# A two-block sequence model on one core: weight sums of the seven-product up projection formed by accumulating DMAs

## The chip, the cores and the metric

The kernel runs on one core of one Trainium2 chip. The metric is the device time of one execution in microseconds (us); several executions of one build are timed and the median is given. Engines are named as in the profile: PE (TensorE), PEld (its weight loads), DVE (VectorE), ACT (ScalarE), POOL (GpSimd), SP (SyncE); a "q" behind a name is that engine's queue of instructions, and DMAs are issued from the queues of SP, ACT and POOL.

## The reference

Two blocks of two layers each on 512 tokens of 1024 features, in float32. The first block has a recurrent layer and an attention layer, which the change doesn't touch. Each layer of the second block ends with the part that matters here, a feed-forward network with a squared ReLU:

```python
    x = x + merged @ w_o
    h2 = rmsnorm(x, norm_mlp)
    return x + jnp.square(jax.nn.relu(h2 @ w_up)) @ w_down
```

`w_up` is 1024 x 4096 and `w_down` 4096 x 1024, both float32, and there are two such layers.

## The kernel before

Every float32 operand is split into two float32r parts that add up to it (high part by an ACT copy, line 59 for weights; low part by a DVE subtraction, line 60), and every product is made of three matmuls (high x high, high x low, low x high; lines 254 to 256, `mm3`).

**Weights come as a stream** (`Stream`). An item is one output tile of 128 columns, [128, 1024] float32, 512 KB. It is loaded by SP into a tile of the pool `wraw` (4 buffers), split by ACT and DVE into tiles of `whi` and `wlo` (3 buffers each), and read by PE. A buffer comes free when its last reader is done.

**The up projection** of a layer makes 32 output tiles in 16 pairs. A pair takes seven products of half-size blocks in place of eight (Winograd's variant of Strassen's product): the two weight tiles are cut into four blocks, A11 and A12 (first tile, lower and upper half of the contraction), A21 and A22 (second tile). Besides A11, A12 and A22 as they are, four sums are wanted: S1 = A21 + A22, S2 = S1 - A11, S3 = A11 - A21, S4 = A12 - S2. `_emit_sums` forms them with four [128, 512] additions (lines 96, 98, 101 and 104): by POOL for the first four pairs of a layer (`pooled`), by DVE for the other twelve. S1, S2 and S4 stand in the pool `sraw` (2 buffers) and are split into the pool `sums` (tiles `sh`, `sl`, 3 buffers each); S3 overwrites A21 in its `wraw` tile. In names, the stream's number stands before the sum: `sr191S`, `sh191S`, `wr191a`, `wr191b`. The blocks of the activations, T1 to T4 (tiles TH, TL), xH and xL, come from the norm ahead of the up projection (`PairNorm`).

`pair` multiplies in the order A11, A12, S1, S2, S3, S4, A22 (products 1, 2, 5, 6, 7, 3, 4), twelve 256-column matmuls each, and recombines on ACT (copies, lines 395 and 397), DVE (lines 396, 398, 401, 402, 404, 406) and POOL (line 399, `s_up`: one 256-column addition for each pair, on which lines 402 and 404 wait). Behind it stand ReLU times the norm's row (line 1150, DVE), the square (line 1151, ACT) and the split into aH and aL (lines 269 and 270).

**Groups.** Four pairs and eight tiles of the down projection (`dn`, 512-column matmuls) make a group; a layer has four groups, the kernel eight. The first two down tiles multiply parts 0 to 5 of the contraction first (36 matmuls), and then parts 6 and 7, which the last pair makes.

**Order.** PE's order is written out by hand. The orders of the other engines, and of the DMAs on their queues, come from a list scheduler that works with its own estimates of time; each engine then runs its list strictly in that order, so that an instruction that waits holds all behind it. `W.next()` emits the weights of the pair after the one it returns (`ahead` is 1 for pairs).

Of the kernel before, what the change touches and what calls it, by code (L numbers as in the profile page):

```python
# [7 lines left out]
F32 = mybir.dt.float32  # L8
# [7 lines left out]
P = 128  # L16
S = 512
D = 1024
KD = D // P
EPS = 1e-6  # L20
# [10 lines left out]
# columns of the packed per-partition vectors  # L31
# [16 lines left out]
class Stream:  # L48
    """Weights in order of use: load, split into two float32r parts that add up exactly."""

    def __init__(self, tc, raw, hi, lo, items, ahead):
        self.nc, self.raw, self.hi, self.lo = tc.nc, raw, hi, lo
        self.items, self.ahead = items, ahead
        self.done, self.taken = [], 0
        self.sums = self.sraw = None
        self.pooled = 0  # so many of the next sums go to GpSimd, while VectorE has much else to do
# [5 lines left out]
    def _emit_sums(self, i, s1, s2):  # L62
        """Weights of two output tiles in Winograd's seven forms, each a pair of [P, 4, P] parts.

        Rows of the 2 x 2 blocks A are the output tiles, columns the halves of the contraction.
        """
        nc, hw, nh = self.nc, KD * P, KD * P // 2
        eng = nc.gpsimd if self.pooled > 0 else nc.vector
        self.pooled -= 1
        r1 = self.raw.tile([P, hw], F32, tag="wraw", name=f"wr{i}a")  # L70
        r2 = self.raw.tile([P, hw], F32, tag="wraw", name=f"wr{i}b")
        nc.sync.dma_start(r1, s1)
        nc.sync.dma_start(r2, s2)
        a11, a12, a21, a22 = r1[:, :nh], r1[:, nh:], r2[:, :nh], r2[:, nh:]
# [16 lines left out]
        def sraw(nm):  # L91
            return self.sraw.tile([P, nh], F32, tag="sraw", name=f"sr{i}{nm}")

        whole(("A11", "A12"), r1)
        v1 = sraw("S1")
        eng.tensor_add(v1, a21, a22)
        half("S1", v1)
        eng.tensor_sub(a21, a11, a21)
        whole(("S3", "A22"), r2)
        v2 = sraw("S2")  # L100
        eng.tensor_sub(v2, v1, a11)
        half("S2", v2)
        v4 = sraw("S4")
        eng.tensor_sub(v4, a12, v2)
        half("S4", v4)
# [35 lines left out]
class Map:  # L141
    """A pool whose tags stand for tags of other pools."""
# [9 lines left out]
def build(tc, A, out, dbg=None):  # L152
# [3 lines left out]
    with ctx:  # L156
# [116 lines left out]
        def rsqrt_row(dst, src, scale, tp, tag, load=True):  # L273
            """dst = 1 / sqrt(src * scale + EPS), all float32 of one shape: a first value and a Newton step."""
# [12 lines left out]
        def colsum(acc, tp, tag):  # L287
            """Sum of acc over its partitions, on every partition of a PSUM tile."""
# [8 lines left out]
        class Norm:  # L297
            """Splits x * gain as tiles of x come, and sums their squares."""
# [39 lines left out]
        class PairNorm:  # L338
            """As Norm, with Winograd's forms of x * gain: blocks are halves of the features by halves of the tokens."""
# [27 lines left out]
        def pair(tag, forms, cp, cs, first=False):  # L367
            """Two output tiles [P, S] by Winograd's variant of Strassen's product."""
# [12 lines left out]
            steps = ((1, "A11", "B11"), (2, "A12", "B21"), (5, "S1", "T1"), (6, "S2", "T2"))  # L381
# [16 lines left out]
            dve.tensor_add(z, ps[6], s1)  # L398
            pool.tensor_add(s5, s5, z)  # L399
            prod(7, "S3", "T3")  # L400
            dve.tensor_add(z, ps[7], z)
            dve.tensor_add(c2[:, S2:], ps[7], s5)
            prod(3, "S4", "B22")
            dve.tensor_add(c1[:, S2:], ps[3], s5)
            prod(4, "A22", "T4")
            dve.tensor_add(c2[:, :S2], ps[4], z)
# [10 lines left out]
        def columns(r, tag):  # L417
            """[P, 4]: the row r with tokens on partitions."""
# [7 lines left out]
        def log1p_small(dst, e, tp, shape, tag):  # L426
            """log(1 + e) for e in [0, 1], to float32 accuracy in relative terms."""
# [15 lines left out]
        def trig():  # L443
            """cos and sin of position * frequency, [frequency twice, token]: sin on partitions ..63, cos on 64.. first."""
# [23 lines left out]
            # rows 64.. multiply the second half into the first one  # L468
            act.mul(sind[64:], sind[:64], -1.0)

        # =====================================================================
        # layer 1: LRU
        # =====================================================================
        with ExitStack() as lc:
# [13 lines left out]
            # softplus(-a_param), times -4 and -8  # L488
# [132 lines left out]
        # =====================================================================  # L621
        # layer 2: forgetting attention
        # =====================================================================
        with ExitStack() as lc:
# [20 lines left out]
            # keys: high parts twice; low parts, and over the other half of the rows the cumulated forget gates  # L645
# [5 lines left out]
            def fox_forget(ft):  # L651
                """Log sigmoid of the forget gates, [token, block of tokens and head], in two parts."""
# [19 lines left out]
            # P^T of a head, key block kb from column 384 * kb + query on  # L672
# [187 lines left out]
        # =====================================================================  # L860
        # second block
        # =====================================================================
# [61 lines left out]
        for li in range(2):  # L924
# [254 lines left out]
            lay.close()  # L1179


# [1 line left out]
def lay_out(inputs):  # L1183
    import numpy as np

# [96 lines left out]
```

## Time and profile before

| | |
|---|---|
| time, median of 3 runs | 2293.59 us (2293.43 to 2295.14) |
| profiled execution | 2293.59 us, all of it inside its span of 2293.6 us |
| PE busy | 2238.3 us (98%) |
| DVE / ACT / POOL busy | 1543.9 (67%) / 1065.4 (46%) / 369.0 us (16%) |
| DMA | 210.42 MB, mean 92 GB/s, queue of SP 28.1% of the 16 engines |
| PE share of the chain that ended last | 82% |

Of a group of instructions the profile gives busy time, the mean of one, and the idle time of its engine just before with what ended that idle time. A DMA issue is given with its size and the time from issue to landing.

### The profile page before, as it was taken

The numbers are of one execution on the slowest core, as the hardware profiler recorded it, in microseconds if no ns is written. First come the engines' busy times: TensorE is split into PE (matmuls) and PEld (weight loads), VectorE is DVE, ScalarE is ACT, GpSimd is POOL, SyncE is SP. The second block draws the span as 40 slices with busy tenths as digits, with TensorE's granted clock in tenths as the row PEclk, the third lists the DMA queues.
The fourth block names the chain that finished last, engine by engine and source line by source line (L and its number), as shares of the span: only waits on it lengthen the run. The fifth ranks groups of instructions, "written<-read, shape, count | busy, mean of one in ns | idle before, by whom it ended". The sixth has DMA issues, their size and how long they took to land.

```text
span 2293.6 us, 30071 instructions
## 1 busy us (share of the span) xinstructions
PE 2238.3 (98%) x11818; PEld 1909.7 (83%) x11818; DVE 1543.9 (67%) x2256; ACT 1065.4 (46%) x1629; POOL 369.0 (16%) x269
## 2 busy tenths in 40 slices
PE   8898999999999999999999999999999999999998
PEld 6687778887888888887998998988888887998996
DVE  7987877777776445448875774766345548875774
ACT  5666577765556222235543444556222225443443
POOL 3434211113211000003310112211000004210112
PEclk9999999999999999999999999999999999999999
DMA  4133222222222332332332333222333322333331
GB/s 153 64 99 97 90 65 74 65 74 80 81 94 74 101 100 94 98 95 74 110 102 95 100 109 99 89 89 80 96 97 95 98 92 83 101 103 100 97 107 55
DMA packets 62509, 210.42 MB, mean 92 GB/s; under 512 B 6944, under 2 KB 11424, under 8 KB 62368
## 3 DMA queue, kind: packets, MB, share of 16 engines
q1 hardware_dynamic: 59552, 204.43, 28.1%
q10 hardware_dynamic: 2672, 3.81, 0.6%
q8 instruction: 93, 1.52, 0.3%
q14 instruction: 48, 0.39, 0.1%
q0 software_dynamic: 144, 0.26, 0.0%
HBM read 206.37 MB, written 2.10 MB: 91 GB/s over the span
## 4 chain that ended last, share of the span: by engine, by line
PE 82%; DVE 5%; ACT 1%; issue 1%; POOL 0%; DVEq 0%; ACTq 0%; POOLq 0%
PE dn L255 5%; PE dn L256 5%; PE dn L254 5%; PE up L255 4%; PE up L256 4%; PE up L254 4%; PE ro L981 1%; PE wr L256 1%; PE wc L254 1%; PE wc L256 1%; PE wc L255 1%; PE wr L255 1%; PE wr L254 1%; PE ga L254 1%; PE ga L256 1%
## 5 line engine op out<-in xcount | busy, mean ns | idle before, releaser
L59 ACT CAST wh<-wr 128x1024 fp32r<-128x1024 f32 (+2 forms) x332 | 337.2, 1017 | 707.9 <-PE dn L255 120.5
L60 DVE TENSOR_TENSOR wl<-wr,wh 128x1024 fp32r<-128x1024 f32 (+2 forms) x332 | 398.5, 1202 | 49.7 <-ACT wh L59 47.9
L255 PE MATMUL dn<-aL,wh 128*128 128x512 f32 x488 | 192.9, 395 | 0.3 <-DVE aL L270 0.3
L256 PE MATMUL dn<-aH,wl 128*128 128x512 f32 x488 | 192.8, 395 | 0.0
L254 PE MATMUL dn<-aH,wh 128*128 128x512 f32 x488 | 192.7, 395 | 0.0
L399 POOL TENSOR_TENSOR s_up<-s_up,sz_up 128x256 f32<-128x256 f32 x32 | 52.6, 1644 | 473.5 <-DVE sz_up L398 163.8
L1169 DVE TENSOR_TENSOR x<-dn,x 128x512 f32<-128x512 f32 x61 | 42.0, 689 | 111.1 <-PE dn L256 110.8
L255 PEld LDWEIGHTS dn<-aL,wh 128*128 128x128 f32 x488 | 91.5, 187 | 22.7 <-DVE aL L270 0.7
L256 PEld LDWEIGHTS dn<-aH,wl 128*128 128x128 f32 x488 | 91.5, 187 | 22.3
L254 PEld LDWEIGHTS dn<-aH,wh 128*128 128x128 f32 x488 | 91.5, 187 | 22.1
L326 POOL TENSOR_TENSOR nacc_m<-nacc_m,nsq_m 128x512 f32<-128x512 f32 x14 | 21.0, 1499 | 486.4 <-ACT nsq_m L325 486.4
L256 PE MATMUL rv<-wh,xL 128*128 128x256 f32 x256 | 72.4, 283 | 0.0
L255 PE MATMUL rv<-wl,xH 128*128 128x256 f32 x256 | 72.4, 283 | 0.0
L254 PE MATMUL rv<-wh,xH 128*128 128x256 f32 x256 | 72.4, 283 | 0.0
L1151 ACT ACTIVATE c_up<-c_up 128x512 f32<-128x512 f32 x64 | 40.5, 633 | 35.0 <-DVE c_up L1150 34.7
L254 PE MATMUL wo<-mH,wh 128*128 128x512 f32 x128 | 51.1, 399 | 0.0
L256 PE MATMUL wr<-yrH,wl 128*128 128x512 f32 x128 | 51.1, 399 | 0.0
L254 PE MATMUL wc<-zH,wh 128*128 128x512 f32 x128 | 50.6, 396 | 0.0
L256 PE MATMUL wc<-zH,wl 128*128 128x512 f32 x128 | 50.6, 395 | 0.0
L255 PE MATMUL wc<-zL,wh 128*128 128x512 f32 x128 | 50.5, 395 | 0.0
L255 PE MATMUL wr<-yrL,wh 128*128 128x512 f32 x128 | 50.5, 394 | 0.0
L256 PE MATMUL wo<-mH,wl 128*128 128x512 f32 x128 | 50.4, 394 | 0.0
(1561 smaller groups left out, 7144.5 us busy)
## 6 DMA issues: line engine op xcount, KB each, us to landing
wr<-in_w_in SPq DMA_DIRECT2D x112, 512.0 KB, 3.5
wr<-in_w_down SPq DMA_DIRECT2D x64, 512.0 KB, 3.5
wr<-in_fox_w_in SPq DMA_DIRECT2D x24, 512.0 KB, 3.5
wr<-in_lru_w_in SPq DMA_DIRECT2D x23, 512.0 KB, 3.6
wr<-in_w_v SPq DMA_DIRECT2D x16, 512.0 KB, 3.5
wr<-in_w_ret_out SPq DMA_DIRECT2D x16, 512.0 KB, 3.5
wr<-in_w_conv_out SPq DMA_DIRECT2D x16, 512.0 KB, 3.6
wr<-in_w_o SPq DMA_DIRECT2D x16, 512.0 KB, 3.5
```

Of the source, the lines that this page charges most:

```text
L59: self.nc.scalar.copy(h, src)
L60: self.nc.vector.tensor_sub(l, src, h.bitcast(F32))
L254: pe.matmul(ps, wH, aH, start=start, stop=False)
L255: pe.matmul(ps, wH, aL, start=False, stop=False)
L256: pe.matmul(ps, wL, aH, start=False, stop=stop)
L326: (dve if j > 5 and acc is self.acc2 else pool).tensor_add(acc, acc, sq)
L399: pool.tensor_add(s5, s5, z)
L981: pe.matmul(po[i][:, q0:], vp[:, kb, vs], sp_[:, so], start=n == 0, stop=n == 11)
L1151: act.activation(t, t, AF.Square)
L1169: dve.tensor_add(x[:, j], ps, x[:, j])
```

## The change

The four additions of a pair go away. The raw sums are formed while the weights are loaded: POOL issues DMAs that add their source onto a tile that is already in SBUF (`accum_op=add`). Since these only add, the second output tile is computed with its sign turned, so that all four sums are plain additions: V1 = A21 + A22, V3 = A21 + A11, V2 = A11 + V1, V4 = A12 + V2, and the recombination subtracts where it added. `sraw` has 3 buffers in place of 2, one each for V1, V2 and V4 of a pair. A pair now has five loads by SP (two of 512 KB, three of 256 KB) and four accumulating DMAs by POOL of 256 KB each; two of these read HBM (V1, V3), and two read the sum before them in SBUF (V2 reads V1, V4 reads V2). `pooled` is gone. The remaining lines of the diff take comments out, and shift line numbers behind `_emit_sums` by one.

```diff
@@ Stream._emit_sums
-        eng = nc.gpsimd if self.pooled > 0 else nc.vector
-        self.pooled -= 1
-        r1 = self.raw.tile([P, hw], F32, tag="wraw", name=f"wr{i}a")
-        r2 = self.raw.tile([P, hw], F32, tag="wraw", name=f"wr{i}b")
-        nc.sync.dma_start(r1, s1)
-        nc.sync.dma_start(r2, s2)
-        a11, a12, a21, a22 = r1[:, :nh], r1[:, nh:], r2[:, :nh], r2[:, nh:]
...
+        def load(nm, src):
+            t = self.sraw.tile([P, nh], F32, tag="sraw", name=f"sr{i}{nm}")
+            nc.sync.dma_start(t, src)
+            return t
+
+        add = mybir.AluOpType.add
+        r1 = self.raw.tile([P, hw], F32, tag="wraw", name=f"wr{i}a")
+        nc.sync.dma_start(r1, s1)
+        v1 = load("V1", s2[:, :nh])
+        nc.gpsimd.dma_start(v1, s2[:, nh:], accum_op=add)
+        r2 = self.raw.tile([P, hw], F32, tag="wraw", name=f"wr{i}b")
+        nc.sync.dma_start(r2, s2)
+        nc.gpsimd.dma_start(r2[:, :nh], s1[:, :nh], accum_op=add)
+        v2 = load("V2", s1[:, :nh])
+        nc.gpsimd.dma_start(v2, v1, accum_op=add)
+        v4 = load("V4", s1[:, nh:])
+        nc.gpsimd.dma_start(v4, v2, accum_op=add)
         whole(("A11", "A12"), r1)
-        v1 = sraw("S1")
-        eng.tensor_add(v1, a21, a22)
-        half("S1", v1)
-        eng.tensor_sub(a21, a11, a21)
-        whole(("S3", "A22"), r2)
-        v2 = sraw("S2")
-        eng.tensor_sub(v2, v1, a11)
-        half("S2", v2)
-        v4 = sraw("S4")
-        eng.tensor_sub(v4, a12, v2)
-        half("S4", v4)
+        half("V1", v1)
+        half("V2", v2)
+        whole(("V3", "A22"), r2)
+        half("V4", v4)
@@ pair
-            dve.tensor_add(z, ps[6], s1)
-            pool.tensor_add(s5, s5, z)
-            prod(7, "S3", "T3")
+            dve.tensor_sub(z, s1, ps[6])
+            pool.tensor_sub(s5, s5, z)
+            prod(7, "V3", "T3")
...
@@ build
-                W.pooled = 4
-                W.sraw = lay.enter_context(tc.tile_pool(name=f"u{li}_r", bufs=2, side="right"))
+                W.sraw = lay.enter_context(tc.tile_pool(name=f"u{li}_r", bufs=3, side="right"))
```

The change moves instructions on three engines. POOL first, in the second group of a layer (its pairs have the stream's numbers 189 to 192, the next group's first pair 201; `s_up_1_0`, `_2`, `_4`, `_6` are the additions of line 399 for its four pairs). Before:

```order
L399 TENSOR_TENSOR s_up_1_0_9934<-s_up_1_0_9934,sz_up_1_0_9935 128x256
L399 TENSOR_TENSOR s_up_1_2_10082<-s_up_1_2_10082,sz_up_1_2_10083 128x256
L399 TENSOR_TENSOR s_up_1_4_10230<-s_up_1_4_10230,sz_up_1_4_10231 128x256
L399 TENSOR_TENSOR s_up_1_6_10353<-s_up_1_6_10353,sz_up_1_6_10354 128x256
L399 TENSOR_TENSOR s_up_2_0_10782<-s_up_2_0_10782,sz_up_2_0_10783 128x256
```

Now, in the same place (L97 adds A11 onto `wr192b`, L94 forms V1, L99 V2, L101 V4):

```order
L400 TENSOR_TENSOR s_up_1_0_9952<-s_up_1_0_9952,sz_up_1_0_9953 128x256
L97 DMA wr192b<-in_w_up 128x512
L94 DMA sr191V_10018<-in_w_up 128x512
L99 DMA sr191V_10024<-sr191V_10018 128x512
L101 DMA sr191V_10027<-sr191V_10024 128x512
L400 TENSOR_TENSOR s_up_1_2_10103<-s_up_1_2_10103,sz_up_1_2_10104 128x256
L94 DMA sr192V_10169<-in_w_up 128x512
L99 DMA sr192V_10175<-sr192V_10169 128x512
L101 DMA sr192V_10178<-sr192V_10175 128x512
L400 TENSOR_TENSOR s_up_1_4_10254<-s_up_1_4_10254,sz_up_1_4_10255 128x256
L94 DMA sr201V_10641<-in_w_up 128x512
L99 DMA sr201V_10647<-sr201V_10641 128x512
```

POOL had one addition for each pair and nothing between; now three or four DMA issues stand between two of them, of which each waits for the DMA before it to land. The next row of POOL is `s_up_1_6`. The sums of pairs 189 and 190 stand ahead of these rows, in the time of the down projection before.

DVE in the same group, at its last pair (`c_up_1_6`; `sl201V` are low parts of the next group's first pair). Before:

```order
L398 TENSOR_TENSOR sz_up_1_6_10354<-up_1_6_6_10339,s_up_1_6_10352 128x256
L270 TENSOR_TENSOR aL_1_4_10285<-c_up_1_4_10232,aH_1_4_10284 128x512
L401 TENSOR_TENSOR sz_up_1_6_10354<-up_1_6_7_10362,sz_up_1_6_10354 128x256
L402 TENSOR_TENSOR c_up_1_6_10356<-up_1_6_7_10362,s_up_1_6_10353 128x256
L404 TENSOR_TENSOR c_up_1_6_10355<-up_1_6_3_10377,s_up_1_6_10353 128x256
```

Now:

```order
L399 TENSOR_TENSOR sz_up_1_6_10378<-s_up_1_6_10376,up_1_6_6_10363 128x256
L59 TENSOR_TENSOR sl201V_10658<-sr201V_10641,sh201V_10657 128x512
L59 TENSOR_TENSOR sl201V_10662<-sr201V_10647,sh201V_10661 128x512
L402 TENSOR_TENSOR sz_up_1_6_10378<-up_1_6_7_10386,sz_up_1_6_10378 128x256
L403 TENSOR_TENSOR c_up_1_6_10380<-s_up_1_6_10377,up_1_6_7_10386 128x256
L405 TENSOR_TENSOR c_up_1_6_10379<-up_1_6_3_10401,s_up_1_6_10377 128x256
```

The splits of the next group's V1 and V2 have moved ahead of the last pair's recombination.

SP in the same stretch. Before:

```order
L73 DMA wr191b<-in_w_up 128x1024
L72 DMA wr192a<-in_w_up 128x1024
L73 DMA wr192b<-in_w_up 128x1024
L120 DMA wr_10294<-in_w_down 128x1024
L120 DMA wr_10417<-in_w_down 128x1024
```

Now:

```order
L92 DMA wr192a<-in_w_up 128x1024
L96 DMA wr192b<-in_w_up 128x1024
L87 DMA sr191V_10018<-in_w_up 128x512
L87 DMA sr191V_10024<-in_w_up 128x512
L87 DMA sr191V_10027<-in_w_up 128x512
L121 DMA wr_10318<-in_w_down 128x1024
L121 DMA wr_10441<-in_w_down 128x1024
L87 DMA sr192V_10169<-in_w_up 128x512
```

Three loads of 256 KB for each pair have come in, behind the loads of the tiles that the pair after it needs whole and among those of the down projection.

## Rows read from the trace of the kernel before

**Rows 1.** The page: busy time of each engine over the span.

```profile
PE 2238.3 (98%) x11818; PEld 1909.7 (83%) x11818; DVE 1543.9 (67%) x2256; ACT 1065.4 (46%) x1629; POOL 369.0 (16%) x269
```

**Rows 2.** Waits of PE, 1040 to 1460 us (engine, line, releaser: total, times, longest).

```profile
PE up L255 <- DVE xL L270: 2.2, 2, 1.4
PE up L254 <- ACT xH L269: 2.1, 1, 2.1
```

**Rows 3.** Windows: one group's pairs and downs (busy by engine, clock, DMA share, GB/s).

```profile
1167.78:1207.65 39.87, 39.87 (x338) 39.87 (x336) 36.20 (x62) 23.13 (x37) 7.23 (x4) 1.00 0.34 106
1207.65:1252.44 44.79, 44.79 (x194) 35.98 (x193) 23.46 (x31) 12.61 (x16) 0.00 (x0) 1.00 0.29 94
```

**Rows 4.** Timeline of PE: first matmuls of pairs 1 and 2, first of the downs.

```profile
1167.78 0.28 PE L254 MATMUL up<-xH,wh189A 128*128 128x256 f32 x1
...
1177.75 0.28 PE L254 MATMUL up<-xH,wh190A 128*128 128x256 f32 x1
...
1207.65 0.39 PE L254 MATMUL dn<-aH,wh 128*128 128x512 f32 x1
```

**Rows 5.** Timeline of DVE in that group (start, length, line, tiles, idle before).

```profile
1171.82 1.23 DVE L60 TENSOR_TENSOR wl190S<-wr190b,wh190S 128x1024 fp32r<-128x1024 f32 x1 [0.47 <-ACT wh190S L59]
...
1188.39 0.68 DVE L96 TENSOR_TENSOR sr192S<-wr192b 128x512 f32<-128x512 f32 x1
...
1198.99 0.42 DVE L401 TENSOR_TENSOR sz_up<-up,sz_up 128x256 f32<-128x256 f32 x1 [0.64 <-POOL s_up L399]
1199.33 0.41 DVE L402 TENSOR_TENSOR c_up<-up,s_up 128x256 f32<-128x256 f32 x1
1199.66 0.41 DVE L404 TENSOR_TENSOR c_up<-up,s_up 128x256 f32<-128x256 f32 x1
...
1201.46 0.68 DVE L60 TENSOR_TENSOR sl192S<-sr192S,sh192S 128x512 fp32r<-128x512 f32 x1
1202.06 0.68 DVE L1150 SCALAR_TENSOR_TENSOR c_up<-c_up,r_m 128x512 f32<-128x512 f32 x1
```

**Rows 6.** Timeline of POOL: sums of pair 177, and line 399 of pair 189.

```profile
1053.56 1.31 POOL L96 TENSOR_TENSOR sr177S<-wr177b 128x512 f32<-128x512 f32 x1 [2.43 <-DMA wr177b<-in_w_up]
1054.94 2.16 POOL L98 TENSOR_TENSOR wr177b<-wr177a,wr177b 128x512 f32<-128x512 f32 x1
...
1174.27 1.04 POOL L399 TENSOR_TENSOR s_up<-s_up,sz_up 128x256 f32<-128x256 f32 x1 [49.44 <-ACT sh190S L59]
```

**Rows 7.** Timeline of DVE ahead of the up projection and in its first products.

```profile
1074.46 1.78 DVE L270 TENSOR_TENSOR xL<-xgb_m,xH 128x512 fp32r<-128x512 f32 x1
...
1084.69 0.68 DVE L270 TENSOR_TENSOR xL<-xgb_m,xH 128x512 fp32r<-128x512 f32 x1
```

**Rows 8.** POOL's one DMA: time on the engine itself (ns min/median/max).

```profile
L643 POOL DMA_DIRECT2D tri<-in_tri x1: 741/741/741, 263.5 to 263.5; - x1
```

**Rows 9.** DMA issues (tiles, queue, count, KB each, us from issue to landing).

```profile
wr<-in_w_down SPq DMA_DIRECT2D x64, 512.0 KB, 3.5
...
wr<-in_lru_wab SPq DMA_DIRECT2D x12, 128.0 KB, 2.0
...
wr192b<-in_w_up SPq DMA_DIRECT2D x1, 512.0 KB, 4.4
...
wr<-in_fox_vf SPq DMA_DIRECT2D x1, 272.0 KB, 2.7
...
tri<-in_tri POOLq DMA_DIRECT2D x1, 256.0 KB, 3.2
```

**Rows 10.** Timeline of ACT in that group: split, square, split of the result.

```profile
1182.13 0.62 ACT L59 CAST sh191S<-sr191S 128x512 fp32r<-128x512 f32 x1 [0.37 <-PE up L255]
...
1182.92 0.64 ACT L1151 ACTIVATE c_up<-c_up 128x512 f32<-128x512 f32 x1
...
1184.08 0.62 ACT L269 CAST aH<-c_up 128x512 fp32r<-128x512 f32 x1
```

**Rows 11.** Timeline of DVE: waits on ACT of one dependency.

```profile
1163.27 1.22 DVE L60 TENSOR_TENSOR wl189S<-wr189b,wh189S 128x1024 fp32r<-128x1024 f32 x1 [0.20 <-ACT wh189S L59]
```

More of the change, by code (lines that the diff above doesn't have):

```diff
@@ L55, in __init__ @@
         self.sums = self.sraw = None
-        self.pooled = 0
     def _split(self, h, l, src):
@@ L89, in half @@
             out[nm] = tuple(t.rearrange("p (a b) -> p a b", b=P) for t in (h, l))
-        def sraw(nm):
-            return self.sraw.tile([P, nh], F32, tag="sraw", name=f"sr{i}{nm}")
-        whole(("A11", "A12"), r1)
-        v1 = sraw("S1")
-        eng.tensor_add(v1, a21, a22)
-        half("S1", v1)
-        eng.tensor_sub(a21, a11, a21)
-        whole(("S3", "A22"), r2)
-        v2 = sraw("S2")
-        eng.tensor_sub(v2, v1, a11)
-        half("S2", v2)
-        v4 = sraw("S4")
-        eng.tensor_sub(v4, a12, v2)
-        half("S4", v4)
+        def load(nm, src):
[14 more added lines that the diff above has]
+        nc.gpsimd.dma_start(v4, v2, accum_op=add)
+        whole(("A11", "A12"), r1)
+        half("V1", v1)
+        half("V2", v2)
+        whole(("V3", "A22"), r2)
+        half("V4", v4)
         self.done.append(out)
@@ L379, in prod @@
                     mm3(ps[n], h[:, k], l[:, k], bh, bl, k == 0, stop and k == 3)
-            steps = ((1, "A11", "B11"), (2, "A12", "B21"), (5, "S1", "T1"), (6, "S2", "T2"))
+            steps = ((1, "A11", "B11"), (2, "A12", "B21"), (5, "V1", "T1"), (6, "V2", "T2"))
             if first:
@@ L397, in pair @@
             act.copy(s5, ps[5])
-            dve.tensor_add(z, ps[6], s1)
-            pool.tensor_add(s5, s5, z)
-            prod(7, "S3", "T3")
+            dve.tensor_sub(z, s1, ps[6])
+            pool.tensor_sub(s5, s5, z)
+            prod(7, "V3", "T3")
             dve.tensor_add(z, ps[7], z)
-            dve.tensor_add(c2[:, S2:], ps[7], s5)
-            prod(3, "S4", "B22")
-            dve.tensor_add(c1[:, S2:], ps[3], s5)
+            dve.tensor_sub(c2[:, S2:], s5, ps[7])
+            prod(3, "V4", "B22")
+            dve.tensor_sub(c1[:, S2:], ps[3], s5)
             prod(4, "A22", "T4")
-            dve.tensor_add(c2[:, :S2], ps[4], z)
+            dve.tensor_sub(c2[:, :S2], ps[4], z)
             return c1, c2
```

## The prediction

> **What bounds the kernel now.** I read the page first: PE is busy for 98% of the span, and no other engine passes 67% [rows 1]. Then the waits of PE, where the up and down projections run: one layer loses 4.3 us in two lines at its first pair, where PE waits for the norm's last split (xH, xL), and nearly nothing elsewhere [rows 2]; the second layer's list reads the same. So the stage that the change touches runs at PE's pace already, and the most that it can give back is 2 x 4.3 = 8.6 us. Then the clock of one group: pairs start 9.97 us apart (1167.78, 1177.75), four of them take 39.87 us, and the eight down tiles after them 44.8 us, at full granted clock [rows 3, 4]. A product is a seventh of a pair, 1.42 us; a down matmul takes 44.8 / 192 = 0.233 us. The question is thus not what the additions cost, but whether the sums, made in the new way, still arrive before PE asks for them.
>
> **Removed: no gain beyond the 8.6 us.** On DVE go 12 pairs x 4 x 0.68 us for each layer [rows 5], 65 us in both, but DVE is busy for only 36.2 of a group's 39.9 us of pairs and half of the downs [rows 3], and PE waits for none of it. On POOL go 16 additions of 1.3 to 2.2 us for each layer [rows 6]; beside them DVE's instructions stretch (the same split of xL takes 1.78 us there and 0.68 us once POOL is quiet [rows 7]). That could shorten the chain to the first pair and give back part of the 4.3 us in each layer. I count it at zero: the 4.3 us hang on the last tiles of x, whose splits already ran at 0.68 us [rows 7]. The recombination keeps its instructions, with subtractions for additions.
>
> **Added: three more loads by SP and four accumulating DMAs by POOL for each pair.** Issuing costs POOL 0.74 us each [rows 8], 3 us of a pair's 10 us on an engine that is busy for 7.2 of 39.9 us [rows 3]; SP's issues lie beside other work. What counts is latency, since the sums form a chain: V2 adds V1 and V4 adds V2, so POOL, which runs its list in order, stands still after each issue until the sum before has landed. Buffers close the loop. V1, V2 and V4 have one `sraw` buffer each, so the next pair's V1 can be loaded only when this pair's V2 DMA, its last reader, has landed. From one pair's V1 to the next it thus takes two accumulating DMAs (A each) and one load (L): **2A + L against PE's 9.97 us**.
>
> L: 128 KB land in 2.0 us, 272 KB in 2.7 and 512 KB in 3.5 [rows 9], so 256 KB alone in 2.6; with another load on the same 16 DMA engines 512 KB took 4.4 in place of 3.5 [rows 9], so 2.6 + 0.9 = 3.5 under load. I take 3.5, since two more loads are issued right behind.
> A: no row shows an accumulating DMA. The nearest is POOL's one plain DMA, also 256 KB, at 3.2 us [rows 9]. An addition must also read its destination; 256 KB more cost 0.85 us between 272 and 512 KB, so 4.05 alone, and 4.95 with a load beside it. I take **A = 5.0**. The lower end is 3.2 (the second read and the sharing cost nothing). As upper end I take two whole transfers one after the other, 6.4, and 7.3 if each also meets a load; nothing in the trace forbids more.
>
> The Trainium skill (Collectives: The Full Stack, The bandwidth ceiling) says that an addition in the DMA engines costs no cycles of its own but needs two source reads on one ring, and so doubles the read traffic. No row here shows it. By it the second read is paid in full, which is where I stand; without it A would be 4.1 under load, and by the formulas below PE would not stall.
>
> **The chain in one group**, from the start of its pair 1 (1167.78), by POOL's new order. The sums of pairs 1 and 2 are made in the downs before. POOL begins on pair 3 when `wr192b` has been loaded: its buffer is free after the split of `wr190b` (1171.82 + 1.23 [rows 5], so 5.3), the load takes 3.5, and the DMA onto it is issued first (0.74 [rows 8]): 9.5. (The addition of line 399 of pair 1 is over at 7.5 by then [rows 6].) Then
> - V1 and V2 of pair 3 land at 9.5 + 2A, V1 of pair 4 is loaded and its V1, V2 and V4 land at 9.5 + 5A + L. A split takes 0.62 + 0.68 [rows 5, 10], and eight dependencies cost 0.2 each [rows 11]. PE wants V4 of pair 4, its sixth product, at 3 x 9.97 + 5 x 1.42 = 37.0. Late by **x1 = 5A + L - 24.6**.
> - DVE's list now holds the splits of V1 and V2 of the next group's pair ahead of the recombination of pair 4. V2 there lands at 9.5 + 6A + 2L. Behind it: split 1.3, lines 402 to 405 and 1150 at 1.8 [rows 5], square and split on ACT 1.3 [rows 10], ten dependencies 2.0. PE wants part 6 of the contraction after four pairs and the 36 matmuls that don't need it, at 39.9 + 8.4 = 48.3. Late by **x2 = 6A + 2L - 32.4**; x1 is within it.
>
> With A = 5.0 and L = 3.5: x1 = 3.9, x2 = 4.6. Three groups of a layer lose 4.6 us; the last has no next pair and loses 3.9. That is 17.7 us for each layer, 35 us for both. The downs (44.8 us, with four sums to make, 4A + L and three short DMAs) let each group start afresh. **The sum:** 2293.6 + 35 = **2329 us**. The profiled execution took 2293.59 us, all of it span, and is the median itself.
>
> DMA throughput is no bound over a whole group: its 8 MB become 15, and 4 x 1 MB of second reads; at today's share of 0.29 to 0.34 for a hundred GB/s [rows 3] that is some 0.7 of the engines' time. But it makes the sharing that I priced likely.
>
> **Rivals.** 0.2%, 4.6 us, is about what a measurement of this kernel tells from no change.
> 1. *The transfers stay hidden* (no change). x2 is negative for A below 4.2 with L = 3.5, and below 4.4 with L = 3.0. For it: the plain DMA took 3.2 us [rows 9], V2 and V4 read SBUF, not HBM, and PE need only keep up for two pairs of a group. Against: each DMA must read twice and there are three times as many issues in flight. Time: 2293 us. The Trainium skill (DMA: Bandwidth & Descriptors, Anatomy of one DMA) gives a POOL DMA 2.0 us plus its bytes at 436 GB/s, 2.6 us for 256 KB. The row shows 3.2, POOL's issue in it, and is used; by the page x2 would be far below zero, and this rival would come true.
> 2. *The additions were in the way after all* (faster). POOL's additions stretch DVE's instructions ahead of the first pair [rows 7]; without them x's last splits come sooner, and more than half of the 8.6 us goes, with A as low as in rival 1. Time: 2287 us. Against: those last splits were not stretched.
> 3. *The accumulating DMA is dear* (much slower). At A = 6.4, x1 = 10.9 and x2 = 13.0: 50 us for each layer, 2393 us; at A = 7.3, 2435 us. For it: nothing here shows how the DMA engines add. Against: most of the 3.2 us is latency (128 KB already take 2.0), which two reads in one DMA pay once.
> 4. *The norm's sum comes late.* POOL's list before the first pair mixes the norm's seven additions (line 326) with eleven of these DMAs; the norm's last addition stands behind a DMA onto `wr179b`, and PE's column sum after pair 1 waits for it. It decides if that DMA's load comes over 10 us after the first pair's start; then each layer loses some 3 us more. It is in the range.
>
> **How the numbers follow.** Stalls as forecast (A from 4.5 to 5.7, 2306 to 2361 us): 0.52. Rival 3, with rival 4: 0.23. Rival 1: 0.19. Rival 2: 0.06. So faster 0.06, same 0.19, slower 0.75. The range reaches from rival 1, less a little of the 8.6 us, to rival 3's dearer end: 2291 to 2430.
>
> **What would show it.** Right: PE waits at the sixth product of pairs 3 and 4 (for the splits of V4) and at `dn`'s second part (for aH), a few us in each group; POOL's accumulating DMAs land in about 5 us; the V1 loads are issued just as V2 of the pair before lands; and every line 400 but the first of a group starts late. Wrong: accumulating DMAs that land in under 4.2 us with PE's list of waits as short as today; or stalls that stand at SP's loads for the downs, which I held to be covered; or an engine other than PE at over nine tenths in the groups.

## The result, and the profile after

The changed kernel takes **2381.11 us** (median of 4 runs, 2376.24 to 2385.26) beside 2294.36 us of the kernel before on the same chip: 1.0375 times as long, interval 1.036 to 1.039. It is slower by 87 us; 35 were forecast. The profiled execution has a span of 2380.0 us.

The page, busy time of each engine, and POOL's DMA queue (packets, MB, share of 16 DMA engines):

```profile
PE 2273.4 (96%) x11818; PEld 1932.6 (81%) x11818; DVE 1496.0 (63%) x2160; ACT 1053.9 (44%) x1629; POOL 408.0 (17%) x365
...
q0 software_dynamic: 18576, 33.82, 8.5%
```

Against [rows 1], PE is busy for 35.1 us more with the same 11818 matmuls, and it idles for 106.6 us (2380.0 - 2273.4) where it idled for 55.3: 51.3 us more. So the 86 us between the two profiled executions are 51 of waiting and 35 of slower matmuls. The waits of PE (engine, line, releaser: total, times, longest):

```profile
PE dn L255 <- ACT aH L270: 21.3, 7, 5.1
...
PE up L255 <- ACT sh192V L58: 2.1, 1, 2.1
...
PE up L257 <- DVE sl192V L59: 1.5, 1, 1.5
```

At `dn`'s second part they stand where the prediction had put them. In the last pair of a group it had named V4, the sixth product; they stand at V2, the fourth (192 is shown; the longest such wait is 4.6 us, at 204). At V4 PE waits for only 3.8 us in all eight groups, nearly all of it in the first group of a layer. Windows of the group of [rows 3] (busy by engine, clock, DMA share, GB/s), its pairs and its downs, and four short ones around the wait at V2 of pair 192:

```profile
1178.99:1225.67 46.68, 43.02 (x337) 42.40 (x336) 33.59 (x51) 22.49 (x38) 11.74 (x14) 0.93 0.70 182
1225.67:1275.05 49.38, 46.66 (x195) 36.85 (x193) 19.84 (x26) 11.77 (x15) 6.02 (x7) 0.97 0.58 149
...
1209.45:1213.00 3.55, 3.55 (x32) 3.55 (x31) 2.75 (x5) 1.37 (x4) 0.86 (x1) 1.00 0.94 247
1213.00:1216.00 3.00, 0.90 (x7) 0.69 (x7) 0.21 (x1) 0.86 (x2) 0.42 (x1) 1.00 0.39 137
1216.00:1219.00 3.00, 1.50 (x7) 1.30 (x7) 2.96 (x5) 0.70 (x1) 1.73 (x3) 0.54 0.78 175
1219.00:1222.00 3.00, 3.00 (x16) 3.00 (x15) 2.97 (x5) 2.77 (x6) 0.36 (x1) 0.50 0.63 112
```

The pairs take 46.68 us in place of 39.87, the downs 49.38 in place of 44.79: 11.4 us in one group. Right behind the wait the granted clock is 0.5, the lower of the two levels (1.2 GHz), for some 7 us. The DMA share has doubled, from 0.34 and 0.29 [rows 3] to 0.70 and 0.58; in the window where it is highest, 0.94, the clock is full.

PE in that stretch: the two waits at V2, the first matmul of V4 (`xH,sh192V`), and the wait at `dn` (start, length, line, tiles, idle before):

```profile
1215.81 0.39 PE L255 MATMUL up<-TH,sh192V 128*128 128x256 f32 x1 [2.10 <-ACT sh192V L58]
...
1217.81 0.58 PE L257 MATMUL up<-TH,sl192V 128*128 128x256 f32 x1 [1.50 <-DVE sl192V L59]
...
1222.67 0.41 PE L255 MATMUL up<-xH,sh192V 128*128 128x256 f32 x1
...
1236.96 0.79 PE L255 MATMUL dn<-aH,wh 128*128 128x512 f32 x1 [2.72 <-ACT aH L270]
```

And POOL's list, the chain of sums of pairs 191, 192 and 201 (L94 V1, L99 V2, L101 V4):

```profile
1188.99 0.88 POOL L97 DMA_DIRECT2D wr192b<-in_w_up  x1 [2.25 <-DMA wr192b<-in_w_up]
1189.58 1.19 POOL L94 DMA_DIRECT2D sr191V<-in_w_up  x1
1197.61 0.87 POOL L99 DMA_DIRECT2D sr191V<-sr191V  x1 [6.84 <-DMA sr191V<-in_w_up]
1201.44 0.87 POOL L101 DMA_DIRECT2D sr191V<-sr191V  x1 [2.97 <-issue]
...
1203.86 0.89 POOL L94 DMA_DIRECT2D sr192V<-in_w_up  x1 [0.78 <-DMA sr192V<-in_w_up]
1209.52 0.86 POOL L99 DMA_DIRECT2D sr192V<-sr192V  x1 [4.77 <-DVE aL L271]
1215.58 0.86 POOL L101 DMA_DIRECT2D sr192V<-sr192V  x1 [5.21 <-DMA sr192V<-sr192V]
...
1218.47 0.89 POOL L94 DMA_DIRECT2D sr201V<-in_w_up  x1 [1.27 <-DMA sr201V<-in_w_up]
1223.96 0.86 POOL L99 DMA_DIRECT2D sr201V<-sr201V  x1 [4.60 <-DMA sr201V<-in_w_up]
```

From a V1 issue to its V2 issue it takes 8.03, 5.66 and 5.49 us. How long the DMAs of this chain took from issue to landing (tiles, queue, count, KB, us): V1 of the three pairs, V2 of the three pairs, and the loads of the tiles of V1 for the second and third pair:

```profile
sr191V<-in_w_up POOLq DMA_DIRECT2D x1, 256.0 KB, 7.5
sr192V<-in_w_up POOLq DMA_DIRECT2D x1, 256.0 KB, 4.0
sr201V<-in_w_up POOLq DMA_DIRECT2D x1, 256.0 KB, 4.4
...
sr191V<-sr191V POOLq DMA_DIRECT2D x1, 256.0 KB, 3.3
...
sr192V<-sr192V POOLq DMA_DIRECT2D x1, 256.0 KB, 5.5
...
sr201V<-sr201V POOLq DMA_DIRECT2D x1, 256.0 KB, 7.0
...
sr192V<-in_w_up SPq DMA_DIRECT2D x1, 256.0 KB, 2.6
...
sr201V<-in_w_up SPq DMA_DIRECT2D x1, 256.0 KB, 2.7
```

SP's own waits from 1179 to 1280 us show the loop of buffers, loads by L87 that wait for a DMA of the pair before. Of the two waits in the row, one is the load of V1's tile, which waits for V2 of the pair before to land, and one is the load of V2's tile, which waits for V4 of the pair before:

```profile
SPq L87 <- DMA sr191V<-sr191V: 10.1, 2, 6.3
```

What hangs on V2 of pair 201 is seen on ACT and DVE: the split of the next group's V2 waits for its DMA, and the last pair's recombination (L402) comes behind it.

```profile
1231.01 0.62 ACT L58 CAST sh201V<-sr201V 128x512 fp32r<-128x512 f32 x1 [7.04 <-DMA sr201V<-sr201V]
...
1231.66 0.69 DVE L59 TENSOR_TENSOR sl201V<-sr201V,sh201V 128x512 fp32r<-128x512 f32 x1 [5.79 <-ACT sh201V L58]
1232.27 0.42 DVE L402 TENSOR_TENSOR sz_up<-up,sz_up 128x256 f32<-128x256 f32 x1
```

### The profile page after: what moved, and what is told of

Same layout as the page of the kernel before. It is cut to its first block, busy times and chain, and to the rows that moved or that the text cites. A ratio compares the mean times of both kernels' runs of the same rounds, so it can differ in the third digit from the quotient of the medians.

```text
span 2380.0 us, 30571 instructions
## 1 busy us (share of the span) xinstructions
PE 2273.4 (96%) x11818; PEld 1932.6 (81%) x11818; DVE 1496.0 (63%) x2160; ACT 1053.9 (44%) x1629; POOL 408.0 (17%) x365
## 2 busy tenths in 40 slices
DMA packets 94769, 269.18 MB, mean 113 GB/s; under 512 B 10528, under 2 KB 15008, under 8 KB 94624
## 3 DMA queue, kind: packets, MB, share of 16 engines
q0 software_dynamic: 18576, 33.82, 8.5%
q8 instruction: 93, 1.52, 0.3%
## 5 line engine op out<-in xcount | busy, mean ns | idle before, releaser
L255 PE MATMUL wr<-yrH,wh 128*128 128x512 f32 x128 | 50.2, 392 | 0.0
L256 PE MATMUL wo<-mL,wh 128*128 128x512 f32 x128 | 50.2, 392 | 0.0
L255 PE MATMUL ga<-xH,wh 128*128 128x512 f32 x128 | 50.1, 391 | 0.0
```

The lines of the kernel that those rows point to most:

```text
L255: pe.matmul(ps, wH, aH, start=start, stop=False)
L256: pe.matmul(ps, wH, aL, start=False, stop=False)
```

## The experiments

Ratios are to the kernel before, run on the same chip.

**1. A fourth buffer.**

```diff
-W.sraw = lay.enter_context(tc.tile_pool(name=f"u{li}_r", bufs=3, side="right"))
+W.sraw = lay.enter_context(tc.tile_pool(name=f"u{li}_r", bufs=4, side="right"))
```

> One more buffer for V1, V2 and V4 (4 in place of 3), so that the load of the next pair's V1 no longer waits until this pair's V2 DMA has landed. Theory (the buffer loop sets the pace: 2A + L from one pair's V1 to the next, with A of 3.4 to 6.2 us and L of 3.0 to 4.7 us in the trace of the change): the load is out of the loop, V4 of the group's last pair comes about L, some 4 us, sooner, the waits of 3.6 us in one group at product 6 (V2) go, and the half-clock stretch behind them goes too. Time 2300 to 2345 us. Rival 1 (POOL's list in order is the bound, not the buffer: each accumulating DMA waits for the landing of the one before, whenever the load came): less than a third goes, 2350 to 2381 us. Rival 2 (DVE's order: the next group's V1 and V2 splits stand ahead of the last pair's recombination): waits at product 6 go, but the 21 us at the second part of the down projection stay with their clock, 2330 to 2350 us, and they are the longest line of PE's waits.

Measured: 2348.26 us, 1.0247 (1.021 to 1.028); the profiled execution was the slowest of its four, 2364.26 us. The waits at V2 go, from 28 us over all groups to 0.5, as the theory and rival 2 say. Others come at V4, where the prediction had looked for them: 2.0 and 0.2 us in pair 192, 5.6 in all. And PE's longest line of waits has grown:

```profile
PE dn L255 <- ACT aH L270: 28.9, 6, 6.7
```

DMAs of two pairs are now issued half a microsecond apart (V4 of pair 191 at 1198.94, V1 of 192 at 1199.48), and they land later; V4's landing times, whose median was 3.6:

```profile
DMA to landing us min/median/max: 3.3/5.5/9.9
```

The loop of buffers is a cause: 33 us go. The time lies between the theory's 2345 and rival 1's 2350 us; rival 2 has it in its range and has the place of the rest right.

**2. The addition left out.** The sums are not formed: the DMAs copy.

```diff
-nc.gpsimd.dma_start(v2, v1, accum_op=add)
+nc.gpsimd.dma_start(v2, v1)
```

(and so for V1, V3, V4)

> The four POOL DMAs of a pair stay where they are and read what they read, but copy instead of adding: the four sums are left out. Theory (the second read of an accumulating DMA is what made A, the landing time of 256 KB, 3.4 to 6.2 us where a plain POOL DMA took 3.2): A falls to 3.0 to 3.5 us, the loop to about 10.5 us for a pair, and most waits in the groups go: 2295 to 2330 us. Rival (A is fixed cost, and sharing of the 16 DMA engines with the loads; the addition itself costs little): A falls by less than 0.5 us at the median, and the time by less than a third of the loss, 2350 to 2381 us.

Measured: 2309.60 us, 1.0069 (1.0049 to 1.0088): 72 of the 87 us are gone. The landing times of V1 and V2 (L94 and L99) in the changed kernel:

```profile
DMA to landing us min/median/max: 3.9/4.5/8.6
...
DMA to landing us min/median/max: 3.3/4.7/7.3
```

The same of the copies:

```profile
DMA to landing us min/median/max: 3.2/3.7/5.0
...
DMA to landing us min/median/max: 2.2/3.8/5.6
```

And POOL's queue of the copies, which had 18576 packets and 8.5%:

```profile
q0 software_dynamic: 10384, 33.82, 4.3%
```

The same megabytes go in fewer packets and half the engine time. The size of the packets alone doesn't explain the half: at the median a packet of 2 KB that adds took 178 ns, and one of SP's loads of the same size 84. Of V1's and V2's landing 0.8 and 0.9 us go at the median, 3.6 and 1.7 at the worst, and each is a link of a chain of six. The theory holds, with medians a little above its 3.5. Of the 72 us some 61 go in the groups; the other 11 are gained ahead of them, where the second pairs of the two layers start that much sooner, in all, than in the change.

**3. Filler matmuls where PE waits.**

```diff
+                    if st[0] == 6 and fill:
...
+                        for k in range(8):
...
+                            mm3(ps[6], h[:, k % 4], l[:, k % 4], bh, bl, k == 0, k == 7)
...
+                            for k in range(4):
+                                mm3(pf, h[:, k], l[:, k], ah[k][0], ah[k][1], k == 0, k == 3)
```

> Matmuls whose result is not used are put into PE's list ahead of two places where it waits: 24 of 256 columns (2.8 us at full clock) ahead of product 6 of each group's last pair, and 12 of 512 columns (2.8 us) ahead of the down projection's second part in three groups of four; 40 us of PE work in both layers. Everything else stays. Theory (the granted clock falls to half after each wait, 3.4 or 6.8 us at a time, which costs 35 us beside the 51 us of waiting): the fillers stand mostly in time that PE waited, half-clock stretches of 68 us shrink to under 25 us, and the time falls to 2340 to 2365 us although PE has 40 us more work. Rival (the clock falls for another reason, as load on the DMA engines or the engines together): the stretches stay, and the time is 2380 to 2400 us.

Measured: 2383.35 us, 1.0382 (1.0365 to 1.0399), no change from the kernel with the DMAs.

```profile
PE 2298.7 (96%) x12082; PEld 1956.8 (82%) x12082; DVE 1492.7 (63%) x2160; ACT 1055.3 (44%) x1629; POOL 406.5 (17%) x365
```

PE is busy for 25.3 us more, though the fillers alone are 40 us: 14 us of half clock are gone, and 19 us of idle time. Yet the time doesn't fall: it is the rival's and not the theory's 2340 to 2365 us, though the slow stretches did shrink. Only 19 of the fillers' 40 us stood in time that PE had waited before, so the run is no clean test of what the clock costs. That the 35 us of slow matmuls are not simply a cost on top is seen in the rows above: PE came to V4 at 1222.67, and DVE had ended the low part of that split at 1222.27. At full clock (0.12 us a matmul, 0.21 here) PE would have come there some 2 us sooner and waited instead.

**4. Two sums by DMA, two by DVE.**

```diff
-v2 = load("V2", s1[:, :nh])
-nc.gpsimd.dma_start(v2, v1, accum_op=add)
-v4 = load("V4", s1[:, nh:])
-nc.gpsimd.dma_start(v4, v2, accum_op=add)
+v2 = self.sraw.tile([P, nh], F32, tag="sraw", name=f"sr{i}V2")
+nc.vector.tensor_add(v2, v1, r1[:, :nh])
+v4 = self.sraw.tile([P, nh], F32, tag="sraw", name=f"sr{i}V4")
+nc.vector.tensor_add(v4, r1[:, nh:], v2)
```

> Only V1 and V3, the sums of two parts of HBM, are formed by accumulating DMAs; V2 and V4, which add a sum to a weight that is in SBUF anyway, are formed by DVE (0.68 us each, 64 more additions, and two loads of 256 KB a pair fewer). Theory (the chain of DMAs, of which each waits for the sum before it, makes the loss): no DMA waits for another DMA's sum but by its own load, PE has no wait over 1 us in the groups, the granted clock stays full there; 2285 to 2300 us. Rival 1 (accumulating DMAs at all: their load on the DMA engines, and POOL held up by them): waits at V1 or V3, 2315 to 2350 us. Rival 2 (DVE becomes late with its 64 additions, as it has V2 ahead of the recombination): waits for DVE at products 6 and 3, 2310 to 2340 us.

Measured: 2304.73 us, 1.0047 (1.0033 to 1.0062). Without DMAs that wait for another DMA's sum 76 us are gone, though an accumulating DMA still takes 4.5 us at the median. The run takes load away as well (235.60 MB moved in place of 269.18), so that by itself it doesn't part the chain from the load. Some 7 of the 76 us stand ahead of the second pairs. The forecast missed by 5 us. What is left has moved to DVE:

```profile
PE dn L256 <- DVE aL L271: 6.3, 5, 2.3
```

**5. The order of the next group's sums.** In the change as it is; `issue_after` queues what it encloses behind a given instruction of the same engine.

```diff
+with ExitStack() as st:
+    for ins in self.behind:
+        st.enter_context(self.tc.issue_after(ins))
...
+if g < 3:
+    W.behind = [*last2, psum_ins[0]]
```

> The change, with one order fixed: POOL's DMAs, ACT's copies and DVE's subtractions for the sums of the next group's first pair stand behind the last pair's addition on POOL and its last split on ACT and DVE, in three groups of four. Nothing else is moved. Theory A (that order is what holds the down projection's second part, 21.3 us of PE's waits, with half-clock stretches behind them): those waits fall under 6 us and the time to 2340 to 2355 us. Theory B (the chain of accumulating DMAs is late for the last pair already, and the order only adds one DMA and one split to it: x2 - x1 is 1 to 2 us a group): the waits at dn go, but waits at product 6 or 3 of the last pair stay or grow, since PE no longer has the half-clock time in which V4 landed; 2360 to 2376 us.

Measured: 2354.59 us, 1.0269 (1.025 to 1.0288). The time is at the upper end of A's range. Both theories have a part: `dn`'s waits for aH are gone in every group (in this one no wait of `dn` is left, and its downs take 45.0 us), as A says; V2's first wait has grown from 2.1 to 3.4 us, as B says. PE's waits from 1160 to 1280 us:

```profile
PE up L260 <- ACT sh192V L59: 3.4, 1, 3.4
```

**6. Order and four buffers together.** Both edits.

> Four buffers for V1, V2 and V4 as in the run with four buffers (2348 us), and the order of the run before this. Theory (with four buffers the last pair's sums are late by only 1 to 3 us, and what is left, 28.9 us of waits at dn with 10 us of half clock behind each, comes from the next pair's DMAs and splits that stand ahead of the last pair's recombination on POOL and DVE): waits at dn under 5 us, 2308 to 2325 us. Rival (the last pair's own sums are late, and dn would wait all the same): 2335 to 2348 us.

Measured: 2316.19 us, 1.0097 (1.0083 to 1.0111). The time is the theory's; 65 of the 87 us are gone with every addition still in the DMAs and as many bytes moved as in the change (269.18 MB), so that the load by itself is not what costs the 65. PE no longer waits for aH. But the waits at `dn` are not under 5 us: its weights, split on ACT and DVE, hold PE for 11.6 us in all, which I have not followed further. In the same stretch:

```profile
PE dn L260 <- ACT wh L59: 1.8, 1, 1.8
```

**7. The price of a wait.** In the kernel before, with a wait at S2 of each last pair.

```diff
+if st[0] == 6 and hold is not None:
...
+    act.copy(e1, ps[5][:, :P])
+    pool.dma_start(e2, e1)
...
+    pe.matmul(ps[6][:, :P], h[:, 0], e2, start=True, stop=True)
```

> The kernel before, with one wait put in on purpose: ahead of the last pair's S2 product in each of the eight groups, PE reads a tile that ACT copies from product 5 and POOL's DMA carries to another place in SBUF; the result of that matmul is not used. Each wait should last 2.3 to 3.0 us. Theory (the granted clock falls to half behind a wait of that length, for 3.4 us or more, and that time is lost too): the time rises by 8 times 4.3 to 6.4 us, to 2328 to 2345 us, and PE's busy time rises by 10 us or more. Rival (the half clock of the change's stretches has another cause, such as its DMA load): only the waits are lost, 8 times 2.3 to 3.0 us, 2312 to 2318 us, and PE's busy time stays at 2238 to 2241 us.

Measured: 2334.33 us, 1.0175 (1.0162 to 1.0189): 40 us for eight waits that sum to 22.7. The page:

```profile
PE 2255.7 (97%) x11826; PEld 1926.5 (83%) x11826; DVE 1547.5 (66%) x2256; ACT 1062.6 (46%) x1637; POOL 376.6 (16%) x277
```

The waits:

```profile
PE up L396 <- DMA h_up<-h_up: 20.0, 7, 3.0
...
PE up L396 <- DVE c_up L414: 2.7, 1, 2.7
```

And windows of one of them (the matmul behind the wait starts at 1207.43):

```profile
1206.00:1209.00 3.00, 1.57 (x8) 1.58 (x9) 0.92 (x3) 2.22 (x4) 0.00 (x0) 0.79 0.21 59
1209.00:1213.00 4.00, 4.00 (x28) 4.00 (x27) 2.77 (x5) 0.36 (x1) 0.73 (x1) 0.73 0.39 129
```

PE's busy time grows by 17.4 us, and 22.7 + 17.4 = 40.1. The DMA share is low here (0.21 and 0.39), so load on the DMA engines is not what lowers the clock in this run: it falls behind the wait. A wait of 2.8 us costs 5.0 where PE alone sets the time.

**8. DMA sums in the first two pairs alone.** V1 and V3 of two pairs a layer by DMA; all else by DVE.

```diff
+if self.byq > 0:
+    v1 = load("V1", s2[:, :nh])
+    nc.gpsimd.dma_start(v1, s2[:, nh:], accum_op=add)
+    nc.sync.dma_start(r2, s2)
+    nc.gpsimd.dma_start(r2[:, :nh], s1[:, :nh], accum_op=add)
+else:
...
+    eng.tensor_add(v1, r2[:, :nh], r2[:, nh:])
+    eng.tensor_add(r2[:, :nh], r1[:, :nh], r2[:, :nh])
...
```

> Accumulating DMAs for V1 and V3 of the first two pairs of each layer alone; every other sum by DVE, none by POOL. In the run with two DMA sums a pair, the second pair of layer 1 began 3.7 us sooner than in the kernel before, and that of layer 2 some 6 us sooner, while the groups behind lost it again. Theory (POOL's additions ahead of the first pair are what made PE wait there; the later sums are best on DVE): 2282 to 2289 us, faster than both kernels. Rival 1 (DVE with all later sums of the first group is late, as POOL had pairs 3 and 4 before): the gain is lost there, 2290 to 2300 us. Rival 2 (what delays the first pair is DVE's or ACT's chain of norm splits): no gain, 2293 to 2296 us.

Measured: **2286.01 us, 0.9964 (0.995 to 0.9978)**, the fastest kernel of the case. PE's waits from 1040 to 1460 us, where [rows 2] had 4.3 us at xH and xL:

```profile
PE dn L267 <- DVE aL L282: 1.3, 1, 1.3
PE up L267 <- DVE xL L282: 0.9, 1, 0.9
```

And DVE's last split of xL in layer 1, which was at 1084.69 [rows 7]:

```profile
1079.85 0.68 DVE L282 TENSOR_TENSOR xL<-xgb_m,xH 128x512 fp32r<-128x512 f32 x1
```

**9 and 10. Controls to it:** all sums by DVE, and DMA sums in the first pair only (`byq` 0 and 1 in place of 2).

> The control to the run with DMA sums in the first two pairs (2286 us): no accumulating DMA and no addition on POOL, all sums of all pairs by DVE, with the change's signs. Theory (the gain came from taking the additions off POOL, which made DVE's and its own work ahead of the first pair slow): the same 2283 to 2289 us. Rival 1 (DVE can't take these eight additions of 0.68 us beside the norm's splits, and the DMAs are what spared it): the gain goes, 2290 to 2297 us. If it is slower than the kernel before, the additions on POOL were right where they were.

> As the run with DMA sums in the first two pairs (2286 us), but only the first pair of each layer has its V1 and V3 from accumulating DMAs; the second pair's are formed by DVE. Theory (what counts is what stands ahead of the first pair's last products; the second pair is wanted 10 us later): within 3 us of it, 2283 to 2289 us. Rival (both pairs' sums stand among the norm's splits on DVE, 1.4 us of additions each): 2288 to 2292 us.

Measured: all by DVE 2289.55 us, 0.9979 (0.997 to 0.9989); first pair only 2287.18 us, 0.9968 (0.9955 to 0.998). So 5 of the 8 us come from taking the additions off POOL, and some 3 from the DMAs (every run with two pairs by DMA, 2284.5 to 2286.9 us, was faster than every run without, 2288.8 to 2294.0, though the two intervals touch). The control lies between its two expectations: DVE can take the sums, at some cost. Whether one pair or two is better can't be told: the intervals overlap.

**11. The DMA by itself.** The kernel before with POOL DMAs of 256 KB beside its downs; `kw` asks for the addition in the second group and is empty in the third.

```diff
...
+for _ in range(2):
+    pool.dma_start(ta_, tb_, **kw)
+    pool.dma_start(tb_, ta_, **kw)
+for _ in range(2):
+    pool.dma_start(ta_, A["w_up0"][0][:, :S], **kw)
```

> The kernel before, with POOL DMAs of 256 KB added beside the down projections of layer 1, where the DMA engines carry only the loads of 512 KB: accumulating ones in the second group (four that read SBUF, one after another, and two that read HBM), plain ones in the same places of the third. Their tiles are read by nothing else. Theory (A of the prediction was too low: an addition costs more than a second read of 0.85 us): accumulating ones take 4.3 to 5.0 us to land here, plain ones 2.8 to 3.3, a difference of 1.3 us or more. Rival (A alone is 4.05 us as taken, and it is sharing with three more loads and two DMAs at a time that made it 5 to 8 us in the change): 3.7 to 4.1 against 3.0 to 3.2 us. The time stays within 0.5% of the kernel before; where a wait of PE appears, it is beside those DMAs.

Measured: 2300.99 us (one run), with a wait of 3.0 us at pair 179 beside the new DMAs: the scheduler set them earlier than meant, among and behind the first group's pairs. These rows have no other work of POOL between them; lines 1168 and 1169 read SBUF, 1171 HBM:

```profile
1099.79 0.86 POOL L1168 DMA_DIRECT2D probea<-probeb  x1
1103.64 0.86 POOL L1169 DMA_DIRECT2D probeb<-probea  x1 [3.00 <-DVE sl179S L60]
...
1129.12 0.56 POOL L1168 DMA_DIRECT2D probea<-probeb  x1 [0.50 <-DMA probeb<-probea]
1131.94 0.54 POOL L1169 DMA_DIRECT2D probeb<-probea  x1 [2.27 <-DMA probea<-probeb]
1134.73 0.54 POOL L1171 DMA_DIRECT2D probea<-in_w_up  x1 [2.24 <-DMA probeb<-probea]
```

The first two accumulate and are 3.85 us apart; the last three copy and are 2.8 us apart. By these rows an addition costs about 1 us, of which 0.3 is POOL's own issue, and A without much beside it is some 3.9 us with its hand-over, near the 4.05 that was taken: the rival's case. Over all twelve DMAs of the run the additions landed in 3.3 to 5.9 us and the copies in 2.5 to 4.5. The longest of each kind were issued within 0.6 us of a load of 512 KB, but so was one of the shortest. That sharing is what makes up to 8 us of a step in the change is thus likely, and not shown.

**12. Two sums by DMA, with the order.** Experiments 4 and 5 in one.

> Two accumulating DMAs a pair (V1 and V3) and two additions by DVE (V2 and V4), as in the run of 2304.7 us, with the order of the two runs before: the next group's first sums stand behind the last pair's recombination, in three groups of four. Theory (what the 10 us over the kernel before are is that order: the next group's first V1 split stands ahead of the last pair's recombination on DVE and holds it while its DMA is on the way): PE's waits at dn go from 9.2 to under 3 us, and with the gain at the first pairs the time is 2284 to 2293 us. Rival (the accumulating DMAs of the last pairs are late by themselves, about 1 us at sl192V and its like, with half clock behind): 2296 to 2304 us.

Measured: 2301.03 us, 1.0028 (1.0017 to 1.0039), in the rival's range: `dn`'s waits fall to 4.6 us, but the last pairs still take 10.4 to 12.1 us in place of 9.97. Even the gentler form loses more in the later groups than it gains at the first pairs.

## Why the prediction was right and wrong

**Right: the direction, the place at `dn`, and the mechanism.** Waits at `dn`'s second part, and loads of V1 behind V2's landing: both are in the trace, and three ways of weakening the chain (a cheaper link, another engine for two links, buffer and order) give back 72, 76 and 65 of the 87 us, the last with every DMA and every byte still there. That DVE's additions cost next to nothing where PE sets the pace is right too (experiment 9, with more of them than before).

**Not worked out: V2.** The last pair's wait was forecast at V4 and stands at V2. By the prediction's own terms V2 of pair 4 would be late by 4A + L - 21.8, which is 1.7 us at its A and L; it priced V4 alone. In the rows V4 has landed and been split while PE waited for V2 and ran at the lower clock behind it.

**Luck: the range.** 2381 us is above the band of 2306 to 2361 that held the forecast, and inside the range only because of rival 3's 2393. But rival 3's reason, a DMA of 6.4 us, is not what the rows show.

**Wrong: the time between a landing and the next start, 0.2 us for each dependency, by which x2 was half of what it is.** x2 was to be 4.6 us in the group of [rows 3]. The new rows give it: from pair 1's start (1178.99) to the first `dn` matmul of the second part (1236.96) are 58.0 us, where PE wanted 48.3. Late by 9.7.
- The first V1 was issued at 10.6 us (1189.58) and not at 9.5: the load of `wr192b` took 4.2 us and not 3.5, and POOL issued its DMA 0.5 us behind the landing.
- The six landings sum to 31.7 us, 5.3 in the mean, where 6A made 30.0; the two loads to 5.3, where 2L made 7.0. Together 37.0, as forecast: "A = 5.0" was slightly low and "L = 3.5" too high, and that the two cancel is luck.
- From the first V1's issue to V2 of pair 201 on ACT (1231.01) are 41.4 us, so 4.4 stand between landings and next starts. From there to PE it took 6.0. All that was counted beside the landings, 4.4 us of work and ten dependencies at 0.2, made 6.4; it is 10.4.

So 1.1 and 4.0 us are what x2 lacked. The 0.2 us had been read from a wait of DVE for ACT [rows 11]. POOL issues some 0.5 us behind the landing that it waits for, and in two of the links more: V2's DMA came 1.6 and 1.1 us behind V1's landing (1209.52 against 1203.86 + 4.0; 1223.96 against 1218.47 + 4.4), though its row can name another engine. By the times in the trace it waited for the load of its own tile, which for pair 192 landed at 1208.95; that load had itself waited for V4 of the pair before, an edge of the buffer loop that the chain left out. In the other groups in the middle of a layer x2 is 9.3 to 12.1 us, and the two loads and the six landings sum to 37 to 40 us there as well.

The price of the addition, 0.85 us, was about right (experiment 11: 1 us). That of sharing, 0.9 us, is not settled by any run: the accumulating DMAs of this one chain land in 3.3 to 7.5 us.

The Trainium skill (Collectives: The Full Stack, The bandwidth ceiling), by which an addition doubles the read traffic, agrees with the queue's engine time: 8.5% against 4.3% of the engines for 33.82 MB. Its formula for a POOL DMA (DMA: Bandwidth & Descriptors, Anatomy of one DMA) gives an estimate of 2.6 us for 256 KB; copies with little beside them were 2.8 us apart here, so that it agrees for such a copy, and says nothing of the addition or the sharing.

**Missing: the clock.** No term stood for it. A wait of 2.8 us costs 5.0 where nothing else binds (experiment 7). In the change the loss is partly cover for the chain's own lateness (the rows of pair 192, experiment 3), and what remains is behind the last wait of a group: from the first `dn` matmul of the second part to the end of the downs are 38.1 us, where 36.4 are their own, so 1.7 are the clock. 9.7 + 1.7 are the 11.4 us of that group. By the starts of the pairs in PE's timeline the six groups with a next pair lose 11.1 to 14.1 us each, where 4.6 were forecast, and the last ones of the two layers 6.8 and 7.5, where 3.9 were; less 3.3 us that the first pairs gain, these are the 86 us. In the two last groups PE waits for 4.3 us, near the forecast; what is above that, 2.5 and 3.2 us, are slower matmuls, so that there nearly all of the miss is the clock.

**Rival 2 was put too low.** I counted POOL's additions ahead of the first pair at zero, since x's last splits already ran at 0.68 us. But they stand, in order, behind stretched ones: of the tile before, DVE's four instructions took 1.27, 1.52, 1.51 and 1.78 us beside POOL's sums, and 0.42, 0.42, 2.12 (beside a POOL addition of the norm) and 0.68 in experiment 8; the last split comes 4.8 us sooner there. Taking the additions off POOL is worth 5 us by itself (experiment 9), and 8 with the first two pairs' sums by DMA. Nor were 8.6 us the most that it could give: that counted the waits and not the slower matmuls behind them. In experiment 8 the second pairs of the two layers start 5.2 and 5.8 us sooner, of which the first groups' downs lose 2.6 again. The changed kernel had some of it: its second pair in the first layer starts at 1090.4 us, 2.1 sooner than before. The Trainium skill (SBUF — State Buffer, SBUF: two separate sides) has DVE instructions with two SBUF inputs and POOL instructions that read SBUF shut each other out; those durations agree.

**Rival 4 did not come.** The column sum behind pair 1 takes 0.62 and 0.47 us in the two layers, 0.46 before.

**Order.** x2 was rightly put above x1, but as a matter of 0.7 us. Taking the next group's sums out of the way is worth 26.5 us (experiment 5), more than 4 us in each of the six groups, with the clock that falls behind `dn`'s wait.

## What to carry to other kernels

Price a chain of DMAs by the step from one issue to the next start under load (here 5.9 us in the mean, of which 5.3 are the landing), not by one landing, and follow every buffer that a DMA in it waits for; a chain of six turns one microsecond into a stall on PE. In this kernel sums of data that is in SBUF anyway were better on an engine with room, and in any case behind, not ahead of, the work that the bottleneck waits for. Add to each new wait of PE the time at the lower clock behind it, but only where no later arrival covers it.

## What was unexpected in the hardware

- An accumulating DMA of 256 KB moved in packets half as large (8192 packets more for 128 DMAs), took twice its queue's engine time, and 0.86 to 0.89 us of POOL's own time to issue (1.19 right behind another), against 0.54 to 0.56 for a copy.
- A wait of PE of under 3 us is followed by some microseconds at the 1.2 GHz level, so that eight of them cost 40 us and not 23. With filler matmuls in such waits (experiment 3) part of the clock came back, and no time was won.
